# A hybrid decoder layer: bias table as one row a head, the first norm's squares off GpSimd, recurrence constants later

## The chip, the core and the metric

The kernel runs on one core of a Trainium2 chip. Its engines are TensorE (PE, matrix products into PSUM), VectorE (DVE), ScalarE (ACT), GpSimd (POOL) and SyncE (SP, which here only issues transfers); they run in parallel and wait for one another by semaphores. Each takes its own instructions strictly in their order. The metric is the device time of one execution in microseconds. The time before is 2371.75 us, the median of three runs (2360.15 to 2379.61).

## The reference, cut to what matters

```python
def reference(x, ...):
    x = x + 0.5 * swiglu(rms_norm(x, ffn1_norm), w_gate, w_up, w_down)      # FFN 1, D=2048, D_FF=5504
    x = x + hybrid_mixer(rms_norm(x, mix_norm), w_in, ...)                  # RG-LRU beside sparse attention
    x = x + 0.5 * swiglu(rms_norm(x, ffn2_norm), ...)                       # FFN 2
    return rms_norm(x, final_norm)

# in the attention, 16 heads of 128, 256 tokens:
bias = rel_bias[t5_causal_bucket(pos - idx)]     # 32 buckets x 16 heads, by relative position
logits = where(valid, q @ k * scale + bias, lowest)

# in the RG-LRU:
log_a = -8.0 * r * softplus(-lam)                # the constants softplus(-lam) do not depend on x
```

All values are float32; one sequence of 256 tokens.

## The kernel before, in words

Activations lie with the channels on partitions (16 row tiles of 128) and the 256 tokens along the free dimension. For full accuracy each weight and each activation is split into a high part and a low part. A weight tile group is 128 x 1024 (eight row tiles, 512 KB): SP loads it into `raw` (3 buffers, L84), ACT writes the high part `whi` (L68), DVE subtracts and writes the low part `wlo` (L69; 3 buffers of each pair), and for each row tile PE makes one 512-wide matmul with the high part (L111) and one 256-wide one with the low part (L112). These two matmuls are called a pair below. So PE needs a new group every eight pairs, and SP, ACT and DVE work ahead by at most three groups. An SP load waits for its `raw` buffer, and what SP issues later stands behind it.

The layer is FFN 1, the mixer (indexer, keys, values, queries with the attention beside them, RG-LRU, gates, output) and FFN 2. FFN 1 runs over 43 column blocks `j` of 128: a gate product `pg` and an up product `pu`, each 16 pairs long; block 0 mixes them by eight row tiles (gate, up, gate, up), because the input tiles `x1hl` are made on the way. `ready1` (L297) makes input tile c: for three of four tiles ACT multiplies the high part (L71) and DVE the low part (L72), for every fourth tile DVE makes both (L300, L301). The sum of squares of the first norm (`Norm.add`, L160) squares 12 of 16 tiles on GpSimd and 4 on ACT, adds on GpSimd, and `sums` (L172) takes it to PE after block 1's gate product; `rstd` spreads the result, and only then can the waiting blocks be evacuated.

`prepare` (L323) stands after block 4 in the program. Its first part makes the recurrence constants `SP2`, `SN4` and `hb` from `vecs` by some thirty operations on 128 x 16 (tile `st`). Its second part multiplies one-hot buckets by the bias table (L354), which gives for each of 16 heads a row `u` of 384 biases by relative position, and writes it to DRAM (`toep`, L358) as a whole Toeplitz block of 128 x 256 for each head, 2 MB from 16 partitions. The mixer reads it back as `TB` in eight transfers (L413), two heads each, and `logits` adds it to the mask on GpSimd (L493, L494).

Order: a scheduler sets each engine's order from the dependences, so an operation without an early dependence can stand far ahead of its place in the program. `held` (L148) makes a zero that is known only when a product is done, to keep later work back.

Of the kernel before, what the change touches and what calls it, by code (L numbers as in the profile page):

```python
# [18 lines left out]
P = 128  # L19
# [24 lines left out]
def hybrid_layer(ctx: ExitStack, tc: tile.TileContext, a, out):  # L44
# [13 lines left out]
    # ---------------------------------------------------------------- helpers  # L58
# [6 lines left out]
    def split(hi, lo, src, scale=None):  # L65
        """hi + lo == src * scale, each in the tensor engine's one-pass form."""
        if scale is None:
            A.activation(hi, src, AF.Copy)  # L68
            V.tensor_tensor(lo, src, hi.bitcast(F32), op=ALU.subtract)  # L69
        else:  # L70
            A.activation(hi, src, AF.Copy, scale=scale)  # L71
            V.scalar_tensor_tensor(lo, src, scale, hi.bitcast(F32), op0=ALU.mult, op1=ALU.subtract)  # L72

    class Stream:
        """Row tiles of a weight in the order of their use, G to a load, cut in two parts."""
# [29 lines left out]
    def part(ps, w, k0, k1, kts, xs):  # L105
        """Row tiles k0..k1 of kts. xs(kt) -> [P, 2 * S] with the two parts of a row tile side by
        side. Left half: high parts; right half: the mixed terms."""
        for k in range(k0, k1):
            x = xs(k)
            hi, lo = w.pop()  # L110
            T.matmul(ps, hi, x, start=(k == 0), stop=False)  # L111
            T.matmul(ps[:, S:], lo, x[:, :S], start=False, stop=(k == kts - 1))  # L112
# [6 lines left out]
    def product1(w, kts, xs):  # L119
        """All terms in the left half."""  # L120
# [9 lines left out]
    def total(ps, M=P):  # L130
        """The sum of both halves."""
# [16 lines left out]
    def held(ps):  # L148
        """A zero that is known once a product is: it keeps later work off an engine until then."""
# [4 lines left out]
    class Norm:  # L154
        """Sums of squares over the channels, tile by tile, then 1 / rms on every partition."""
# [4 lines left out]
        def add(self, t, pool=False):  # L160
            sq = t1("sq")
            if pool:
                GP.tensor_tensor(sq, t, t, op=ALU.mult)
            else:
                A.activation(sq, t, AF.Square)
# [6 lines left out]
        def sums(self, last=None):  # L172
            """1 / rms with the tokens on partitions; last: squares not yet in the sum."""
# [11 lines left out]
            # One Newton step on the table's root.  # L185
# [5 lines left out]
        def spread(self, after=None):  # L191
            """The same on every partition, in PSUM; not before the product after."""
# [16 lines left out]
    # -------------------------------------------------------------- constants  # L209
# [3 lines left out]
    GP.memset(mean, 1.0 / D)  # L213
    vecs = const.tile([P, 8, KT], F32, name="vecs")
# [3 lines left out]
    # ------------------------------------------------------------------- FFN  # L218
    def ffn(wg, wu, wd, xhl, norm, finish, ready=None, early=None, last=None):
# [14 lines left out]
        for j in range(NF):  # L234
# [16 lines left out]
            if j == 0 and ready is not None:  # L251
                for c in range(KT):
                    norm.add(xr[:, c, :], pool=c < 12)
            if j == 1:
                r = norm.rstd(pg)
            if j == 4 and early is not None:
                early()
# [39 lines left out]
    def ready1(c):  # L297
        if c % 4 == 0:
            hi, lo, g = x1hl[:, c, :S], x1hl[:, c, S:], G1[:, c:c + 1]
            V.tensor_scalar(hi, xr[:, c, :], g, None, op0=ALU.mult)  # L300
            V.scalar_tensor_tensor(lo, xr[:, c, :], g, hi.bitcast(F32), op0=ALU.mult, op1=ALU.subtract)  # L301
        else:
            spread(x1hl, c, xr[:, c, :], G1)
# [17 lines left out]
    toep = dram.tile([HEADS, P, S], F32, name="toep")  # L321

    def prepare():  # L323
        # softplus(-lambda): max(-lam, 0) + log1p(e), e = exp(-|lam|), log1p(e) = 2 artanh(e / (2 + e)).
        st = const.tile([P, 6, KT], F32, name="st")
        neg, e, q_, s_, s2, ac = (st[:, i, :] for i in range(6))
        V.tensor_scalar(neg, LAM, -1.0, None, op0=ALU.mult)
# [13 lines left out]
        for k in range(17, 1, -2):  # L341
# [5 lines left out]
        V.tensor_scalar(hb[:, 0, :], BA, 0.5, None, op0=ALU.mult)  # L347
        V.tensor_scalar(hb[:, 1, :], BX, 0.5, None, op0=ALU.mult)

        # Bias by relative position, as rows of a Toeplitz matrix per head.  # L350
# [6 lines left out]
        uw = u[:HEADS, :]  # L357
        nc.sync.dma_start(toep, bass.AP(tensor=uw.tensor, offset=uw.offset + P - 1,  # L358
                                        ap=[list(uw.ap[0]), [-1, P], [1, S]]))
# [3 lines left out]
    # ----------------------------------------------------------------- mixer  # L363
# [18 lines left out]
    # Indexer.  # L382
# [28 lines left out]
    for i in range(8):  # L411
        normed(first[i] if i < 2 else product(W, KT, xs2), r2, IQ[:, i, :])
        nc.sync.dma_start(TB[:, 2 * i:2 * i + 2, :], toep[2 * i:2 * i + 2].rearrange("h q j -> q h j"))  # L413
# [72 lines left out]

    def logits(h):
# [5 lines left out]
        GP.tensor_tensor(tm[:, :P], TB[:, h, P:], MK[:, :P], op=ALU.add)  # L493
        GP.tensor_tensor(tm[:, P:], TB[:, h, :], MK[:, P:P + S], op=ALU.add)  # L494
# [57 lines left out]
    # RG-LRU. With t = tanh(m / 2), m = -log a: a = 2 y - 1, sqrt(1 - a * a) = 2 sqrt(t) y, y = 1 / (1 + t).  # L552
# [5 lines left out]
    def gates():  # L558
# [12 lines left out]
        # One Newton step on (1 + exp(-m)) / 2; y becomes -1 / (1 + t).  # L571
# [77 lines left out]
    # ------------------------------------------------------- FFN, final norm  # L649
# [27 lines left out]
def _buckets():  # L677
    """One-hot buckets of the relative positions 255 - i, i = 0..383 (negative ones as 0)."""
    n = np.maximum(S - 1 - np.arange(3 * P), 0)
# [7 lines left out]
def _tiles(w):  # L687
    """[K, N] -> [groups of G row tiles, 128 (K inside a tile), G * 128], column tile by column tile."""
# [56 lines left out]
```

## Time and profile before

| | |
|---|---|
| median of three runs | 2371.75 us (2360.15 to 2379.61) |
| span of the profiled execution | 2371.8 us |
| PE busy | 2327.9 us, 98% |
| PE weight loads busy | 2037.1 us, 86% |
| DVE busy | 1514.5 us, 64% |
| ACT busy | 1152.8 us, 49% |
| POOL busy | 120.2 us, 5% |
| moved by DMA | 439.54 MB, 185 GB/s in the mean |

An engine's busy share is a mean over all stages. PE is near its limit almost everywhere, so the places that count are those where it is not; the page cuts the span into 40 slices of 59.3 us, and the chain of work that ended last tells what PE waited for. [...]

### The profile page before, as it was taken

To read this page: it belongs to the slowest core of one execution; us is meant where nothing else is said; L and a number is where in the kernel's file an instruction comes from. 1 tells how busy PE (TensorE), PEld (TensorE's weight loads), DVE (VectorE), ACT (ScalarE), POOL (GpSimd) and SP (SyncE) were. 2 spreads that over 40 slices of the span, in tenths; PEclk is the share of its full clock that TensorE was granted. 3 is DMA by queue.
4 is the path that set the end of the run, shared out by engine and by line. 5 is a ranking of instruction groups with operands and counts; after the bars stand their busy time and mean duration, and the time that the engine had idled before them with its cause. 6 is when DMAs were issued, how large, how long until landed. Compare 5 with 4: busy or idle time off the path is not lost.

```text
span 2371.8 us, 34709 instructions
## 1 busy us (share of the span) xinstructions
PE 2327.9 (98%) x13507; PEld 2037.1 (86%) x13507; DVE 1514.5 (64%) x2236; ACT 1152.8 (49%) x1684; POOL 120.2 (5%) x165
## 2 busy tenths in 40 slices
PE   7799999999999999999999999999999999999998
PEld 6688888888888888899888888888888888888887
DVE  7466666665555687778875566676666666664444
ACT  5344444444444445577654444454544444444442
POOL 4000000000000002100000000021000000000000
PEclk9899999999999999999999999999999999999999
DMA  5755555556655644454565656566666666566564
GB/s 198 169 182 186 186 188 186 186 186 196 196 192 193 220 148 160 147 171 157 181 196 188 191 189 188 196 206 201 187 187 191 190 190 191 189 189 193 188 191 146
DMA packets 130580, 439.54 MB, mean 185 GB/s; under 512 B 14416, under 2 KB 25008, under 8 KB 130416
## 3 DMA queue, kind: packets, MB, share of 16 engines
q1 hardware_dynamic: 129360, 434.94, 57.8%
q8 instruction: 105, 1.72, 0.3%
q0 software_dynamic: 912, 2.33, 0.3%
q14 instruction: 59, 0.48, 0.1%
q10 hardware_dynamic: 144, 0.07, 0.0%
HBM read 430.92 MB, written 6.29 MB: 184 GB/s over the span
## 4 chain that ended last, share of the span: by engine, by line
PE 94%; DVE 2%; DMA 2%; ACT 1%; issue 0%; POOL 0%; SPq 0%; DVEq 0%; ACTq 0%
PE mm L111 58%; PE mm L112 30%; PE mm L126 1%; PE mm L125 1%; PE mm L127 1%; DMA raw<-in_wg 1%; DVE wlo L69 1%; DMA raw<-in_w_rg 1%; ACT whi L68 1%; PE aux L426 0%; DVE x1hl L72 0%; PE aux L561 0%; PE aux L562 0%; DVE hst L608 0%; PE aux L491 0%
## 5 line engine op out<-in xcount | busy, mean ns | idle before, releaser
L69 DVE TENSOR_TENSOR wlo<-raw,whi 128x1024 fp32r<-128x1024 f32 (+2 forms) x807 | 988.0, 1224 | 750.9 <-ACT whi L68 748.5
L68 ACT ACTIVATE whi<-raw 128x1024 fp32r<-128x1024 f32 (+2 forms) x807 | 854.2, 1059 | 1144.0 <-PE mm L111 729.4
L111 PE MATMUL mm<-x1hl,whi 128*128 128x512 f32 x1376 | 494.9, 404 | 22.6 <-ACT whi L68 20.6
L111 PE MATMUL mm<-x3hl,whi 128*128 128x512 f32 x1376 | 477.6, 391 | 0.0
L111 PE MATMUL mm<-h,whi 128*128 128x512 f32 x1333 | 466.8, 395 | 0.0
L111 PE MATMUL mm<-x2hl,whi 128*128 128x512 f32 x1280 | 452.8, 396 | 0.0
L112 PE MATMUL mm<-x1hl,wlo 128*128 128x256 f32 x1376 | 390.7, 284 | 5.4 <-DVE wlo L69 5.2
L112 PE MATMUL mm<-x3hl,wlo 128*128 128x256 f32 x1376 | 385.3, 280 | 0.0
L112 PE MATMUL mm<-h,wlo 128*128 128x256 f32 x1333 | 373.8, 280 | 0.0
L112 PE MATMUL mm<-x2hl,wlo 128*128 128x256 f32 x1280 | 359.2, 281 | 4.0 <-DVE wlo L69 3.9
L111 PEld LDWEIGHTS mm<-x1hl,whi 128*128 128x128 f32 x1376 | 262.8, 191 | 89.8 <-ACT whi L68 20.9
L111 PEld LDWEIGHTS mm<-x3hl,whi 128*128 128x128 f32 x1376 | 257.4, 187 | 56.7
L111 PEld LDWEIGHTS mm<-h,whi 128*128 128x128 f32 x1333 | 249.9, 187 | 58.6
L111 PEld LDWEIGHTS mm<-x2hl,whi 128*128 128x128 f32 x1280 | 239.8, 187 | 54.2 <-issue 0.7
L112 PEld LDWEIGHTS mm<-x1hl,wlo 128*128 128x128 f32 x1376 | 263.9, 192 | 7.2 <-DVE wlo L69 7.2
L112 PEld LDWEIGHTS mm<-x3hl,wlo 128*128 128x128 f32 x1376 | 260.0, 189 | 0.0
L112 PEld LDWEIGHTS mm<-h,wlo 128*128 128x128 f32 x1333 | 251.9, 189 | 0.0
L112 PEld LDWEIGHTS mm<-x2hl,wlo 128*128 128x128 f32 x1280 | 241.8, 189 | 7.2 <-DVE wlo L69 6.3
L135 DVE TENSOR_TENSOR tt<-mm,tb 128x256 f32<-128x256 f32 x285 | 119.0, 418 | 6.0 <-ACT tb L133 6.0
L133 ACT ACTIVATE tb<-mm 128x256 f32<-128x256 f32 x285 | 104.2, 366 | 4.4 <-DVE zero L151 2.2
L142 DVE TENSOR_TENSOR tz<-tt,rstd 128x256 f32<-128x256 f32 x224 | 95.0, 424 | 7.0
L111 PE MATMUL mm<-mg,whi 128*128 128x512 f32 x256 | 90.6, 399 | 0.0
(192 smaller groups left out, 2014.2 us busy)
## 6 DMA issues: line engine op xcount, KB each, us to landing
raw<-in_wu SPq DMA_DIRECT2D x172, 512.0 KB, 4.3
raw<-in_wd SPq DMA_DIRECT2D x172, 512.0 KB, 4.2
raw<-in_wg SPq DMA_DIRECT2D x171, 512.0 KB, 4.3
raw<-in_w_q SPq DMA_DIRECT2D x32, 512.0 KB, 3.5
raw<-in_w_rx SPq DMA_DIRECT2D x32, 512.0 KB, 3.5
raw<-in_w_rg SPq DMA_DIRECT2D x32, 512.0 KB, 3.6
raw<-in_w_ga SPq DMA_DIRECT2D x32, 512.0 KB, 3.6
raw<-in_w_pa SPq DMA_DIRECT2D x32, 512.0 KB, 3.6
```

The lines of the kernel that those rows point to most:

```text
L68: A.activation(hi, src, AF.Copy)
L69: V.tensor_tensor(lo, src, hi.bitcast(F32), op=ALU.subtract)
L111: T.matmul(ps, hi, x, start=(k == 0), stop=False)
L112: T.matmul(ps[:, S:], lo, x[:, :S], start=False, stop=(k == kts - 1))
L125: T.matmul(ps[:, :S], hi, x[:, :S], start=(k == 0), stop=False)
L126: T.matmul(ps[:, :S], hi, x[:, S:], start=False, stop=False)
L127: T.matmul(ps[:, :S], lo, x[:, :S], start=False, stop=(k == kts - 1))
L133: A.activation(b[:M], ps[:M, S:], AF.Copy)
L135: V.tensor_tensor(t[:M], ps[:M, :S], b[:M], op=ALU.add)
L142: V.tensor_tensor(o, t, r, op=ALU.mult)
```

## The change

Five edits, beside removed comments:

- `toep` is kept as 384 values for each head (24 KB, written from ACT's queue); the shift by one position for each query row is made when the rows are read back: partition p reads 256 values from position 1 + p. The bucket table now ascends, so a row lies backwards, and GpSimd reads it with step -1 (`back`).
- The first norm's squares are made by ACT, four row tiles at a time, after block 0's gate product (`add_all` with `held`), and added by DVE in halves; GpSimd has no part in it.
- `ready1` makes all 16 tiles on ACT and DVE together.
- `prepare` gets a `held` zero from block 4's gate product, so that its operations can't stand earlier.
- One small activation (`warm`) brings ACT's first table load forward.


```diff
+        def add_all(self, x, after):
+            sq = hl_tile("sqs", F32, (P, KT, S))
+            z = held(after)
+            for c in range(0, KT, 4):
+                A.activation(sq[:, c:c + 4, :], x[:, c:c + 4, :], AF.Square, bias=z)
+            half = KT
+            while half > 2:
+                half //= 2
+                V.tensor_tensor(sq[:, :half, :], sq[:, :half, :], sq[:, half:2 * half, :], op=ALU.add)
+            self.acc = tmp.tile([P, S], F32, name="sqsum", bufs=1)
+            V.tensor_tensor(self.acc, sq[:, 0, :], sq[:, 1, :], op=ALU.add)
...
+    warm = const.tile([P, 1], F32, name="warm")
+    A.activation(warm, mean, AF.Copy)
...
             if j == 0 and ready is not None:
-                for c in range(KT):
-                    norm.add(xr[:, c, :], pool=c < 12)
+                norm.add_all(xr, pg)
...
             if j == 4 and early is not None:
-                early()
+                early(pg)
...
     def ready1(c):
-        if c % 4 == 0:
-            hi, lo, g = x1hl[:, c, :S], x1hl[:, c, S:], G1[:, c:c + 1]
-            V.tensor_scalar(hi, xr[:, c, :], g, None, op0=ALU.mult)
-            V.scalar_tensor_tensor(lo, xr[:, c, :], g, hi.bitcast(F32), op0=ALU.mult, op1=ALU.subtract)
-        else:
-            spread(x1hl, c, xr[:, c, :], G1)
+        spread(x1hl, c, xr[:, c, :], G1)
...
-    toep = dram.tile([HEADS, P, S], F32, name="toep")
-
-    def prepare():
+    toep = dram.tile([HEADS, 3 * P], F32, name="toep")
+
+    def prepare(after):
+        z = held(after)
...
-        V.tensor_scalar(neg, LAM, -1.0, None, op0=ALU.mult)
+        V.tensor_scalar(neg, LAM, -1.0, z, op0=ALU.mult, op1=ALU.add)
...
-        uw = u[:HEADS, :]
-        nc.sync.dma_start(toep, bass.AP(tensor=uw.tensor, offset=uw.offset + P - 1,
-                                        ap=[list(uw.ap[0]), [-1, P], [1, S]]))
+        nc.scalar.dma_start(toep, u[:HEADS])
...
-        nc.sync.dma_start(TB[:, 2 * i:2 * i + 2, :], toep[2 * i:2 * i + 2].rearrange("h q j -> q h j"))
+        rows = toep[2 * i:2 * i + 2]
+        nc.sync.dma_start(TB[:, 2 * i:2 * i + 2, :],
+                          bass.AP(tensor=rows.tensor, offset=rows.offset + 1,
+                                  ap=[[1, P], list(rows.ap[0]), [1, S]]))
...
+    def back(row):
+        n = row.shape[1]
+        return bass.AP(tensor=row.tensor, offset=row.offset + n - 1, ap=[list(row.ap[0]), [-1, n]])
...
-        GP.tensor_tensor(tm[:, :P], TB[:, h, P:], MK[:, :P], op=ALU.add)
-        GP.tensor_tensor(tm[:, P:], TB[:, h, :], MK[:, P:P + S], op=ALU.add)
+        GP.tensor_tensor(tm[:, :P], back(TB[:, h, :P]), MK[:, :P], op=ALU.add)
+        GP.tensor_tensor(tm[:, P:], back(TB[:, h, :]), MK[:, P:P + S], op=ALU.add)
...
-    n = np.maximum(S - 1 - np.arange(3 * P), 0)
+    n = np.maximum(np.arange(3 * P) - P, 0)
```

How the order on the engines moves (line numbers of the changed kernel are up to 15 higher).

DVE at the start, before: between the low parts of the input tiles (L72, L301) and of the weight groups (`wlo`) stand the operations of `prepare` on `st` and the whole tiles made here (L300).

```order
14 L72 SCALAR_TENSOR_TENSOR x1hl<-xr,vecs,x1hl 128x256 x2
15 L330 TENSOR_SCALAR st<-st 128x16
16 L300 TENSOR_SCALAR x1hl<-xr,vecs 128x256
17 L331 RECIPROCAL st<-st 128x16
18 L69 TENSOR_TENSOR wlo<-raw,whi 128x1024
19 L301 SCALAR_TENSOR_TENSOR x1hl<-xr,vecs,x1hl 128x256
20 L72 SCALAR_TENSOR_TENSOR x1hl<-xr,vecs,x1hl 128x256 x3
21 L300 TENSOR_SCALAR x1hl<-xr,vecs 128x256
22 L72 SCALAR_TENSOR_TENSOR x1hl<-xr,vecs,x1hl 128x256
```

DVE at the start, now, from its first instruction to the end of the squares' additions (`sqs`, `sqsum`); `zero` is the held one.

```order
1 L72 SCALAR_TENSOR_TENSOR x1hl<-xr,vecs,x1hl 128x256 x2
2 L69 TENSOR_TENSOR wlo<-raw,whi 128x512 x2
3 L72 SCALAR_TENSOR_TENSOR x1hl<-xr,vecs,x1hl 128x256 x6
4 L69 TENSOR_TENSOR wlo<-raw,whi 128x1024
5 L72 SCALAR_TENSOR_TENSOR x1hl<-xr,vecs,x1hl 128x256 x8
6 L69 TENSOR_TENSOR wlo<-raw,whi 128x1024 x3
7 L151 TENSOR_SCALAR zero<-mm 128x1
8 L169 TENSOR_TENSOR sqs<-sqs 128x2048
9 L69 TENSOR_TENSOR wlo<-raw,whi 128x1024
10 L169 TENSOR_TENSOR sqs<-sqs 128x1024
11 L69 TENSOR_TENSOR wlo<-raw,whi 128x1024
12 L169 TENSOR_TENSOR sqs<-sqs 128x512
```

The operations on `st` and the whole tiles are gone from here, each weight group's low part stands right behind the tiles it needs, and the sixth weight group's low part (row 9) stands behind an addition of 2048 columns.

ACT in the same place, now: the squares stand behind three weight groups and ahead of five.

```order
6 L71 ACTIVATE x1hl<-xr,vecs 128x256 x6
7 L68 ACTIVATE whi<-raw 128x1024
8 L71 ACTIVATE x1hl<-xr,vecs 128x256 x8
9 L68 ACTIVATE whi<-raw 128x1024 x3
10 L165 ACTIVATE sqs<-xr,zero 128x1024 x4
11 L68 ACTIVATE whi<-raw 128x1024 x5
12 L193 ACT_TABLE_LOAD
```

Before, three single squares of 128 x 256 stood here between the loads' high parts.

SP's queue around the table's write, before: it stands between two weight loads of block 7.

```order
26 L84 DMA raw<-in_wu 128x1024 x2
27 L84 DMA raw<-in_wg 128x1024
28 L358 DMA toep<-u 2048x1x256
29 L84 DMA raw<-in_wg 128x1024
30 L84 DMA raw<-in_wu 128x1024 x2
```

Now the write stands on ACT's queue, between a total (L133) and a weight group's high part, and SP's loads follow each other without it.

```order
46 L68 ACTIVATE whi<-raw 128x1024
47 L133 ACTIVATE tb<-mm 128x256
48 L364 DMA toep<-u 16x384
49 L68 ACTIVATE whi<-raw 128x1024
50 L68 ACTIVATE h<-h 128x256
```

PE's order differs in its first 140 rows only; from there on every engine's order is the old one, apart from operations of `prepare` between blocks 4 and 6.

## Rows read from the trace of the kernel before

**Rows 1.** The page: busy us by engine; PE's busy tenths and granted clock in 40 slices.
```profile
PE 2327.9 (98%) x13507; PEld 2037.1 (86%) x13507; DVE 1514.5 (64%) x2236; ACT 1152.8 (49%) x1684; POOL 120.2 (5%) x165
...
PE   7799999999999999999999999999999999999998
...
PEclk9899999999999999999999999999999999999999
```

**Rows 2.** The page: the chain that ended last, shares by engine and by line.
```profile
PE 94%; DVE 2%; DMA 2%; ACT 1%; issue 0%; POOL 0%; SPq 0%; DVEq 0%; ACTq 0%
PE mm L111 58%; PE mm L112 30%; PE mm L126 1%; PE mm L125 1%; PE mm L127 1%; DMA raw<-in_wg 1%; DVE wlo L69 1%; DMA raw<-in_w_rg 1%; ACT whi L68 1%; PE aux L426 0%; DVE x1hl L72 0%; PE aux L561 0%; PE aux L562 0%; DVE hst L608 0%; PE aux L491 0%
```

**Rows 3.** The chain in order of time: start, duration, what.
```profile
80.96 25.40 DMA raw<-in_wg
```

**Rows 4.** Timeline of SP's queue: start, duration, line, transfer.
```profile
79.83 0.70 SPq L358 DMA_DIRECT2D toep<-u  x1
```

**Rows 5.** DMA issues from 60 to 120 us: size, median us to landing.
```profile
raw<-in_wu SPq DMA_DIRECT2D x8, 512.0 KB, 4.4
...
toep<-u SPq DMA_DIRECT2D x1, 2048.0 KB, 24.5
```

**Rows 6.** Timeline of PE around the stall; idle before and releaser in brackets.
```profile
91.62 0.40 PE L111 MATMUL mm<-x1hl,whi 128*128 128x512 f32 x1
...
93.03 0.40 PE L111 MATMUL mm<-x1hl,whi 128*128 128x512 f32 x1
...
107.55 0.79 PE L111 MATMUL mm<-x1hl,whi 128*128 128x512 f32 x1 [14.01 <-ACT whi L68]
...
114.71 0.39 PE L111 MATMUL mm<-x1hl,whi 128*128 128x512 f32 x1
```

**Rows 7.** Stage: length, busy PE, PEld, DVE, ACT, POOL, granted clock, DMA share, GB/s.
```profile
98.00:100.00 2.00, 0.00 (x0) 0.00 (x0) 0.00 (x0) 0.00 (x0) 0.00 (x0) 0.50 0.83 94
```

**Rows 8.** Timeline of DVE at the start.
```profile
6.36 0.48 DVE L72 SCALAR_TENSOR_TENSOR x1hl<-xr,vecs,x1hl 128x256 fp32r<-128x256 f32 x1
6.76 0.68 DVE L69 TENSOR_TENSOR wlo<-raw,whi 128x512 fp32r<-128x512 f32 x1
...
8.61 1.70 DVE L72 SCALAR_TENSOR_TENSOR x1hl<-xr,vecs,x1hl 128x256 fp32r<-128x256 f32 x2
...
15.57 1.59 DVE L69 TENSOR_TENSOR wlo<-raw,whi 128x1024 fp32r<-128x1024 f32 x1
...
24.80 1.21 DVE L69 TENSOR_TENSOR wlo<-raw,whi 128x1024 fp32r<-128x1024 f32 x1
...
32.20 1.22 DVE L342 SCALAR_TENSOR_TENSOR st<-st 128x16 f32<-128x16 f32 x6
```

**Rows 9.** Timeline of PE at the start.
```profile
26.07 0.58 PE L112 MATMUL mm<-x1hl,wlo 128*128 128x256 f32 x1 [3.52 <-DVE wlo L69]
...
29.01 0.43 PE L111 MATMUL mm<-x1hl,whi 128*128 128x512 f32 x1
...
38.58 0.50 PE L178 MATMUL aux<-mean,sqsum 128*128 128x1 f32 x4
```

**Rows 10.** Timeline of ACT at the start.
```profile
7.96 2.30 ACT L71 ACTIVATE x1hl<-xr,vecs 128x256 fp32r<-128x256 f32 x5
...
10.63 1.06 ACT L68 ACTIVATE whi<-raw 128x1024 fp32r<-128x1024 f32 x1 [0.26 <-DMA raw<-in_wu]
```

**Rows 11.** Reads of the table (line 413): time to landing; ACT's timeline during them.
```profile
DMA to landing us min/median/max: 4.1/5.0/6.0
...
799.86 1.06 ACT L68 ACTIVATE whi<-raw 128x1024 fp32r<-128x1024 f32 x1 [2.21 <-DMA raw<-in_w_iq]
```

**Rows 12.** GpSimd's addition (line 494): duration ns min/median/max, starts; a stretch of attention.
```profile
L494 POOL TENSOR_TENSOR misc<-qT,misc x16: 720/738/1791, 897.0 to 989.7; 128x256 f32<-128x256 f32 x16
...
930.00:950.00 20.00, 20.00 (x121) 17.61 (x120) 14.63 (x36) 11.68 (x25) 3.48 (x6) 1.00 0.47 159
```

**Rows 13.** A steady stretch of FFN 1, columns as in rows 7.
```profile
120.00:180.00 60.00, 60.00 (x342) 52.05 (x341) 38.33 (x54) 28.95 (x43) 0.00 (x0) 1.00 0.56 186
```

More of the change, by code (lines that the diff above doesn't have):

```diff
@@ L158, in __init__, with add @@
             self.name, self.acc = name, None
-        def add(self, t, pool=False):
+        def add_all(self, x, after):
[9 more added lines that the diff above has]
+            V.tensor_tensor(self.acc, sq[:, 0, :], sq[:, 1, :], op=ALU.add)
+        def add(self, t):
             sq = t1("sq")
-            if pool:
-                GP.tensor_tensor(sq, t, t, op=ALU.mult)
-            else:
-                A.activation(sq, t, AF.Square)
+            A.activation(sq, t, AF.Square)
             if self.acc is None:
@@ L297, in ready1 @@
     def ready1(c):
-        if c % 4 == 0:
-            hi, lo, g = x1hl[:, c, :S], x1hl[:, c, S:], G1[:, c:c + 1]
-            V.tensor_scalar(hi, xr[:, c, :], g, None, op0=ALU.mult)
-            V.scalar_tensor_tensor(lo, xr[:, c, :], g, hi.bitcast(F32), op0=ALU.mult, op1=ALU.subtract)
-        else:
-            spread(x1hl, c, xr[:, c, :], G1)
+        spread(x1hl, c, xr[:, c, :], G1)
     n2 = Norm("n2")
@@ L346, in prepare @@
         V.tensor_scalar(SN4, SP2, -2.0, None, op0=ALU.mult)
-        V.tensor_scalar(hb[:, 0, :], BA, 0.5, None, op0=ALU.mult)
-        V.tensor_scalar(hb[:, 1, :], BX, 0.5, None, op0=ALU.mult)
+        V.tensor_scalar(hb[:, 0, :], BA, 0.5, z, op0=ALU.mult, op1=ALU.add)
+        V.tensor_scalar(hb[:, 1, :], BX, 0.5, z, op0=ALU.mult, op1=ALU.add)
         bk = t2("bk", 3 * P)
```

## The prediction

> **What bounds the kernel now.** I read the page first, then the chain in order of time, then engine timelines of the places where the chain leaves TensorE. The page says TensorE (PE) is busy 98% of the span [rows 1], and the chain that ended last is 94% PE, nearly all of it the two matmul lines of `part` [rows 2]. So a change elsewhere is worth something only where PE stands still or runs at its lower clock. The slices show where that is: only the first two of the 40 read a PE share of 7; the granted clock is a digit lower in the second. Two causes lie there.
>
> The first is a stall around 100 us. The Toeplitz write is issued on the SP queue at 79.83 us [rows 4], takes 24.5 us for 2 MB, and every weight load normally lands after 4.4 us [rows 5]. The load issued right behind it lands 25.4 us later and stands on the chain [rows 3]. While it runs, the queue moves 94 GB/s and the clock has fallen to 0.50, the lower of its two levels [rows 7]. PE starves from 93.54 us, 13.7 us after the write was issued, until 107.55 us [rows 6].
>
> The second is the start. VectorE (DVE) is on the chain there: GpSimd squares beside it from 4 us on, and a 1024-wide subtraction takes 1.59 us at 15.57 against 1.21 at 24.80, a 256-wide operation 0.85 us at 8.61 against 0.48 at 6.36 [rows 8]. PE waits 3.52 us for the weight split that ends at 26.0 us, reaches the faster cadence at 29.01 and closes its 48th pair (one 512-wide and one 256-wide matmul) at 38.58 us [rows 9].
>
> **The change part by part.** I count against the span of the profiled execution, 2371.8 us, which is the median of the three runs (2371.75).
>
> *The write of 2 MB goes.* A pair costs (93.03-91.62)/4 = 0.352 us at the higher clock. Between 93.54 and 114.71 us, when the fast cadence is back, PE made 10 pairs [rows 6], worth 3.5 us. The rest, 21.2-3.5 = **17.7 us**, is the stall with its slow matmuls; it goes, because a 24 KB write (16 rows of 1.5 KB) on ACT's queue replaces it and no load stands behind that. What ACT pays is one issue of at most 0.7 us (what the SP issue took [rows 4]) plus a wait for the copy of `u`; ACT is busy 28.95 of 60 us in the steady stage [rows 13], so it is covered. Bounds: 17.7 if all goes, 0 if the load behind still waits.
>
> *The start.* DVE loses GpSimd as a neighbour, four 256-wide multiplications, the small operations of `prepare` up to there; ACT takes the four multiplications. I name the weight groups of eight row tiles g0 (gate), g1 (up), g2, g3 (block 0), g4 to g7 (block 1). The data come as before, so g1 is there at 10.6 us [rows 10]. By ACT at 0.46 us a tile and 1.06 us a group, its order gives g1 split by 11.8, eight tiles by 15.5, g2 by 16.5. DVE follows: low part of g1 till 13.0, eight tiles at 0.45 us till 16.6, low part of g2 at 1.2 till **17.8** us, where it was 26.0. From there 32 pairs at 0.352 us make 11.3 us: 29.1. One new wait comes on top. The squares now wait for the gate product, 24 pairs, closed at T = 20.6 us. ACT needs four squares of 1024 columns, 4 x 1.06, and then DVE the first halving addition of 2048 columns: 512 took 0.68 and 1024 took 1.21 [rows 8], so 2.3 us. Behind it on DVE stands the low part of g5, 1.2 us: ready at T+8.0, while PE, having done g3 and g4, wants it at T+5.6. The stall is 2.4 us and pair 48 ends near 31.5 instead of 38.6. Gain **7.0 us**. Bounds: 5.8 if PE shows again the slow pairs that it had from 26.07 to 29.01 (worth 12.5-11.3 = 1.2 us); 2 if the squares and the additions push a second group late as well. I take 7.0, since PE now has work without a gap from about 13 us on.
>
> *The sum of squares later.* The remaining additions (1024, 512, 256 columns: 1.2, 0.7, 0.4 us) lie between weight splits; the sums move 7 pairs back on PE, the diagonal follows at about T+18, and the block that needs the freed PSUM buffer starts at about T+22. Nothing waits; without the 4 us of cover it would cost what is missing.
>
> *`prepare` after block 4's gate product.* Thirty-three operations of 16 columns at 1.22/6 = 0.20 us [rows 8] and a copy, some 7 us, now stand among three to four weight splits; DVE has 60-38.3 of 60 us free [rows 13], 1.0 us in each group of 2.8 us, that is 3 to 4 us, and two groups lie split ahead of PE. I price it **+0.3 us**, bounds 0 and 3.5 (what does not fit, all shown to PE).
>
> *Reading the rows back shifted.* Eight reads of 256 KB land in 4.1 to 6.0 us, and during them one load came late enough to make ACT wait 2.21 us, which PE did not feel [rows 11]. Below: no change. Above: all 2 MB at the write's 94 GB/s, 22 us. The first five (1.25 MB) would block 13.9 us; the write let PE run dry after 13.7; about 3 us of stall, 4 us more for the three that lie between loads, 2 for the clock: **+9**. I take 0, since the reads are nearest to the old reads: same size, same 128 destination rows, same 1 KB runs; only the start within the row is new.
>
> Why the write was slow decides this. The row shows 2 MB from 16 partitions at 94 GB/s. [...]
>
> *Reading backwards on GpSimd.* The 256-wide addition takes 0.74 us [rows 12] and the 128-wide one less; one head is due each 6.2 us (16 starts from 897.0 to 989.7). Step -1 in place of +1: I take no change; the upper bound is a rival.
>
> *Warm-up activation:* the table load leaves ACT's path (1.3 us), but the second half of g0 lands only at 7.3 us: 0.
>
> Sum: -17.7 - 7.0 + 0.3 = -24.4, so **2347.4 us**, 1.0% less.
>
> **Rivals.** *The reads inherit the stall:* the unaligned, overlapping rows are read at the write's rate. For it: every earlier access with an odd start in this trace is that slow write. Against: its 16 source partitions. 2347.4+9 = 2356. *The start gives little:* the chain of squares holds back g5 and g6, or the clock is still low, and 5 us of the 7 are lost: 2352. For it: DVE and ACT are in order, and the splits stand behind the additions. Against: g6 is only 1.2 us of DVE away. *The stall stays* since the write was slow for its queue, not its bytes: only the start is gained, 2365. Against: 94 GB/s fit 2 MB in 24.5 us. *Slower:* GpSimd's reversed read. It decides where the two additions of a head outlast the head's 6.2 us, against about 1.2 us now; at seven times the price, 8.4 us, PE waits 2.2 us in each of 16 heads, 35 us, which gives 2382. Against: nothing in the trace but the absence of a reversed operand; DVE, at 14.63 of 20 us there [rows 12], would suffer as well.
>
> **How the numbers follow.** Forecast 0.66 (2341 to 2353, from the bounds of the start and `prepare`, and about half a per cent of scatter, as the three runs show); reads slow 0.10; start gives little 0.16; stall stays 0.04; GpSimd 0.04. The range 2336 to 2360 takes in the first three and leaves out the last two and the tails. A measurement tells about 1% from no change; 1% faster is 2348.0, inside the forecast: 0.37 of its 0.66 falls below, and 0.07 of the start's and the reads' cases by scatter. Faster 0.44, within 1% 0.52, slower 0.04 (GpSimd).
>
> **What would show it.** In the profile after: no load above about 8 us near 80 us, PE busy without a gap and clock 1.00 from 60 to 118 us; the second low weight part ending near 18 us; pair 48 near 31.5 us with one wait for a weight split of about 2 us ahead of it; no wait of PE among the small operations near 60 to 75 us; reads of the table landing within 7 us and GpSimd's 256-wide addition at 0.74 us. A PE wait near 800 us, or a GpSimd addition of several us, would make the prediction wrong.

## The result and the profile after

| | before | after |
|---|---|---|
| median of four runs | 2371.1 us (2360.15 to 2379.61) | 2342.93 us (2337.04 to 2343.66) |
| ratio, 95% interval | | 0.9897 (0.9856 to 0.9937) |
| span of the profiled execution | 2371.8 us | 2341.3 us |

The forecast was 2347.4, the range 2336 to 2360: the time fell inside, 28 us (1.2%) less than before where 24.4 were expected. The profiled execution lost 30.5 us of span. The page of after stands against [rows 1]: PE is busy 12 us less with the same 13507 matmuls, the first two slices have risen to 8 and 9, and the granted clock of the second is a 9.

```profile
PE 2316.1 (99%) x13507; PEld 2024.9 (86%) x13507; DVE 1505.7 (64%) x2238; ACT 1156.6 (49%) x1689; POOL 95.0 (4%) x137
...
PE   8999999999999999999999999999999999999998
...
PEclk9999999999999999999999999999999999999999
```

**The stall is gone.** Two stretches of after, in the columns of [rows 7]: the slice that held the stall and the very stretch from 93.54 to 114.71 us of [rows 6]. PE is busy throughout and its clock is 1.00.

```profile
59.30:118.60 59.30, 59.30 (x339) 51.06 (x338) 41.66 (x82) 28.28 (x44) 0.00 (x0) 1.00 0.54 187
93.54:114.71 21.17, 21.17 (x124) 18.53 (x123) 13.38 (x19) 10.79 (x16) 0.00 (x0) 1.00 0.56 191
```

The DMA issues of after from 60 to 120 us answer to [rows 5]: the table's write is 24 KB and lands in 2.0 us, and no load is late.

```profile
raw<-in_wg SPq DMA_DIRECT2D x11, 512.0 KB, 3.4
raw<-in_wu SPq DMA_DIRECT2D x10, 512.0 KB, 3.4
toep<-u ACTq DMA_DIRECT2D x1, 24.0 KB, 2.0
```

**The start is shorter, with a wait and a fall of the clock in it.** DVE's timeline of after answers to [rows 8]: the low part of g2 ends at 16.28 + 1.23 = 17.5 us (it was 26.0). The squares follow at 20.6 on ACT, and the first halving addition takes 2.29 us; the next low weight part stands behind it.

```profile
13.11 3.25 DVE L72 SCALAR_TENSOR_TENSOR x1hl<-xr,vecs,x1hl 128x256 fp32r<-128x256 f32 x8
16.28 1.23 DVE L69 TENSOR_TENSOR wlo<-raw,whi 128x1024 fp32r<-128x1024 f32 x1
...
20.42 0.16 DVE L151 TENSOR_SCALAR zero<-mm 128x1 f32<-128x1 f32 x1
24.92 2.29 DVE L169 TENSOR_TENSOR sqs<-sqs 128x2048 f32<-128x2048 f32 x1 [4.34 <-ACT sqs L165]
27.13 1.22 DVE L69 TENSOR_TENSOR wlo<-raw,whi 128x1024 fp32r<-128x1024 f32 x1
```

PE's timeline of after, the two waits behind the squares and the pairs that follow, answers to [rows 9]:

```profile
26.83 0.50 PE L111 MATMUL mm<-x1hl,whi 128*128 128x512 f32 x1 [0.44 <-ACT whi L68]
...
28.40 0.39 PE L112 MATMUL mm<-x1hl,wlo 128*128 128x256 f32 x1 [1.06 <-DVE wlo L69]
...
30.43 0.63 PE L111 MATMUL mm<-x1hl,whi 128*128 128x512 f32 x1
...
31.07 0.63 PE L111 MATMUL mm<-x1hl,whi 128*128 128x512 f32 x1
...
34.49 0.50 PE L188 MATMUL aux<-mean,sqsum 128*128 128x1 f32 x4
...
73.15 0.81 PE L361 MATMUL aux<-bk,rb 32*16 32x384 f32 x2
```

The last row is the bias matmul, the product of buckets and bias table in `prepare`, recorded as two pieces. It stands behind everything that the change moved at the start, and started at 78.40 before:

```profile
78.40 0.81 PE L354 MATMUL aux<-bk,rb 32*16 32x384 f32 x2
```

About 1 us after the second wait the pairs stretch to 0.64 us. Of the stretches from 28 to 34 us (length, PE busy, granted clock, DMA share, GB/s) the middle one is at 0.50 throughout, its neighbours in part; the traces of before and after grant PE 1.00, full speed, or 0.50 and no third level. The 48th pair is done at 32.1 us (38.6 before, 31.5 predicted).

```profile
28.00:30.00 2.00, 1.60 (x8) 0.88 0.21 66
30.00:32.00 2.00, 2.00 (x7) 0.50 0.68 238
32.00:34.00 2.00, 2.00 (x10) 0.77 0.82 274
```

**The reads and GpSimd, which cost nothing** (against [rows 11, 12]): the eight reads of the table, line 420, land in 4.2 to 7.1 us, and the reversed addition, line 508, has the median of before.

```profile
DMA to landing us min/median/max: 4.2/5.9/7.1
```
```profile
L508 POOL TENSOR_TENSOR misc<-qT,misc x16: 724/735/1779, 861.3 to 954.2; 128x256 f32<-128x256 f32 x16
```

**Something that no step named.** PE is busy without a gap at clock 1.00 in each of these stretches, yet it starts a different number of matmuls. First the kernel before, then after; the columns are length, PE busy with its matmuls, clock, DMA share, GB/s.

```profile
200.00:700.00 500.00, 500.00 (x2832) 1.00 0.58 189
1200.00:1500.00 300.00, 300.00 (x1733) 1.00 0.61 192
1700.00:2200.00 500.00, 500.00 (x2886) 1.00 0.61 190
```
```profile
200.00:700.00 500.00, 500.00 (x2886) 1.00 0.58 194
1200.00:1500.00 300.00, 300.00 (x1699) 1.00 0.60 186
1700.00:2200.00 500.00, 500.00 (x2886) 1.00 0.60 190
```

A pair takes 2 x 500/2886 = 0.3465 us in one case and 2 x 500/2832 = 0.3531 in the other. Measured from first to last start the two cadences are 0.3467 and 0.3533 us, in every trace of this study: each stretch of hundreds of us holds one of the two. I call them quick and slow. The first FFN (200 to 700 us) was slow before and is quick after; the gates (1200 to 1500 us) the other way round.

The matmuls are the same in number and order, so the start of the i-th of them can be compared in the two traces, but for the few that the later sums displace. After minus before, in us:

```
first matmul                  -0.6
bias matmul behind block 4    -5.3   start                     -5.3
matmul 500 (stall past)      -23.6   stall (and 0.5 cadence)  -18.3
matmul 4000 (end of FFN 1)   -35.3   cadence in FFN 1         -11.7
matmul 6250 (attention past) -35.5                             -0.2
matmul 9000 (gates past)     -29.0   cadence in the gates      +6.5
matmul 13500                 -30.3   cadence in w_out          -1.4
```

So some 23 us came by the two steps of the prediction, and 7 net by cadence.

### The profile page after: what moved, and what is told of

The parts are those of the page before. It is cut to its first block, busy times and chain, and to the rows that moved or that the text cites. A ratio compares the mean times of both kernels' runs of the same rounds, so it can differ in the third digit from the quotient of the medians.

```text
span 2341.3 us, 34677 instructions
## 1 busy us (share of the span) xinstructions
PE 2316.1 (99%) x13507; PEld 2024.9 (86%) x13507; DVE 1505.7 (64%) x2238; ACT 1156.6 (49%) x1689; POOL 95.0 (4%) x137
## 4 chain that ended last, share of the span: by engine, by line
PE 94%; DVE 3%; DMA 1%; ACT 1%; issue 1%; SPq 0%; POOL 0%; DVEq 0%; ACTq 0%
PE mm L111 58%; PE mm L112 29%; PE mm L126 2%; PE mm L125 2%; PE mm L127 2%; DVE wlo L69 1%; DMA raw<-in_w_rg 1%; ACT whi L68 0%; DMA raw<-in_wu 0%; PE aux L435 0%; PE aux L575 0%; PE aux L576 0%; DVE hst L622 0%; PE aux L505 0%; DMA raw<-in_wg 0%
## 5 line engine op out<-in xcount | busy, mean ns | idle before, releaser
L111 PE MATMUL mm<-x1hl,whi 128*128 128x512 f32 x1376 | 482.5, 397 | 8.1 <-DVE x1hl L72 7.4
L112 PE MATMUL mm<-x1hl,wlo 128*128 128x256 f32 x1376 | 384.2, 279 | 1.8 <-DVE wlo L69 1.8
L133 ACT ACTIVATE tb<-mm 128x256 f32<-128x256 f32 x285 | 104.2, 366 | 2.0 <-DVE zero L151 2.0
L111 PE MATMUL mm<-yat,whi 128*128 128x512 f32 x256 | 91.2, 399 | 0.0
```

The lines of the kernel that those rows point to most:

```text
L133: A.activation(b[:M], ps[:M, S:], AF.Copy)
```

## The experiments

**The two halves apart.** The table alone, from the kernel before:

```diff
-    toep = dram.tile([HEADS, P, S], F32, name="toep")
+    toep = dram.tile([HEADS, 3 * P], F32, name="toep")
...
-        nc.sync.dma_start(toep, bass.AP(tensor=uw.tensor, offset=uw.offset + P - 1,
-                                        ap=[list(uw.ap[0]), [-1, P], [1, S]]))
+        nc.scalar.dma_start(toep, u[:HEADS])
```
(with the shifted reads and GpSimd's reversed ones of the change), and the rest alone, from the kernel after, with the old write, reads and additions put back.

> The kernel before with the bias table edit alone (24 KB write from ACT's queue, shifted reads, backwards additions); squares, prepare and input tiles as before. Theory (the stall is worth 17.7 us, and the loop of pairs keeps one of two cadences, 0.3466 or 0.3533 us a pair, that each interruption of PE sets anew): no wait near 100 us, pair 48 still closed near 38.6 us, span 2371.8-17.7 = 2354, with up to 13 us either way by the cadence in FFN 1 and the gates. Rival (the table edit itself is worth the 30 us, the start nothing): 2342 with a start as before, in every run. Rival (the whole 12 us of faster cadence in FFN 1 comes from the start's edits): slow cadence throughout FFN 1, 2354 or more.

> The changed kernel with the old bias table (2 MB written from 16 partitions on SP's queue, old reads, forward additions); the edits of the start stay. Theory: start gains 5 us as in the changed kernel, the stall of 17.7 us is back near 95 us, span about 2371.8-5 = 2366, with up to 13 us either way by the cadence. Rival (the stall shrinks because the start left more loads ahead): a wait of PE clearly under 14 us, span under 2360.

The table alone: 2360.81 us median, 0.9975 of before (0.995 to 0.9999). The rest alone: 2364.99, 0.9994 (0.9964 to 1.0024). By medians neither half brings much; by their traces each does what it should. With the table alone no stall is left, and the matmuls behind it start 17.8 us earlier against before, matmul 250 to matmul 500. With the rest alone the bias matmul comes 5.9 us earlier and the stall is back in full. The rows: the table alone in two stretches, then PE of the rest alone.

```profile
86.00:114.00 28.00, 28.00 (x161) 1.00 0.54 187
200.00:700.00 500.00, 500.00 (x2832) 1.00 0.55 189
```
```profile
101.65 0.80 PE L111 MATMUL mm<-x1hl,whi 128*128 128x512 f32 x1 [14.29 <-ACT whi L68]
```

The kernel with the table alone ran its first FFN slow (x2832), the rest alone, in its one trace, quick (x2886 in the same stretch). None of the ten runs of the table alone was below 2353.87; before, of which some runs reached 2355, scatters over 25 us, and the rest alone over 22 (2352.4 to 2374.0). Most of these runs have no trace, so how much of the scatter is cadence is not shown; but a difference of two medians can hold it, and a step has to be read where it happens.

**The changed kernel once more**, unchanged, beside those two:

> The changed kernel, not altered, once more. Theory of the two cadences: places in order of instructions as before, but the stretches with 0.3533 us a pair need not be the same ones; if the gates (about 2050 matmuls) are fast this time the span is 7 us shorter, 2334; if FFN 1 is slow it is 13 us longer, 2354. Rival (the cadence is fixed by the program: addresses, buffers, order): every stretch has the cadence of the first profile, span within 1 us of 2341.

2343.27 us (2340.39 to 2343.94), 0.9893 (0.9846 to 0.9941). Its trace has the first FFN quick again and the gates slow again, but not all of it is the same: w_out, quick in the first trace (232 matmuls from 1570 to 1610 us), is slow in this one (228). So the program alone does not fix the cadence everywhere.

**Why the write was slow.** Two kernels from before, each with an edit to the 2 MB write: its source on 128 partitions instead of 16 (`u2`, a 128 x 256 tile that one DVE operation behind block 4 makes for it), or its 128 copies all from the row's start. Both leave out the right bias values.

```diff
-        nc.sync.dma_start(toep, bass.AP(tensor=uw.tensor, offset=uw.offset + P - 1,
-                                        ap=[list(uw.ap[0]), [-1, P], [1, S]]))
+        nc.sync.dma_start(toep.rearrange("h q j -> q h j"), u2[:, None, :].to_broadcast([P, HEADS, S]))
```
```diff
-        nc.sync.dma_start(toep, bass.AP(tensor=uw.tensor, offset=uw.offset + P - 1,
-                                        ap=[list(uw.ap[0]), [-1, P], [1, S]]))
+        nc.sync.dma_start(toep, bass.AP(tensor=uw.tensor, offset=uw.offset,
+                                        ap=[list(uw.ap[0]), [0, P], [1, S]]))
```

> The kernel before, with one edit: the 2 MB Toeplitz write takes its bytes from a 128x256 tile, repeated for the 16 heads, instead of from the 16 rows of u (so the bias values are left out). Same queue, same place, same 2 MB, same 1 KB runs at the destination. Theory A (the write was slow because its source lies on 16 partitions): it lands in 5 to 8 us instead of 24.5, no weight load near 80 to 110 us takes over 12 us, TensorE has no gap there, and the matmuls behind it start some 17 us earlier. Theory B (2 MB on the weights' queue cost this much from any partitions): landing near 24 us, the gap of 14 us stays.

> The kernel before, with one edit: the 2 MB write still comes from the 16 rows of u, but each of the 128 copies starts at the row's start (offset 0, step 0) instead of one element earlier each time, so that every run of 1 KB begins at the same aligned place (the bias values are wrong by it). Theory A (16 source partitions set the rate): landing stays at 24 to 25 us, 94 GB/s, and TensorE's gap of 14 us stays. Theory B (the odd starts set the rate): landing at 5 to 12 us and no gap.

The write among the DMA issues from 60 to 120 us, and a stretch while it runs (columns as in [rows 7]), first from 128 partitions, then from 16 with aligned starts:

```profile
toep<-u SPq DMA_DIRECT2D x1, 2048.0 KB, 8.3
```
```profile
81.00:88.00 7.00, 7.00 (x42) 6.06 (x41) 4.69 (x8) 2.69 (x4) 0.00 (x0) 1.00 1.00 307
```
```profile
toep<-u SPq DMA_DIRECT2D x1, 2048.0 KB, 24.0
```
```profile
96.00:100.00 4.00, 0.00 (x0) 0.00 (x0) 0.00 (x0) 0.00 (x0) 0.00 (x0) 0.60 0.90 94
```

The same 2 MB on the same queue at the same place land in 8.3 us from 128 partitions, while PE never stops, and the matmuls behind start 17.8 us earlier than before. From 16 partitions they take 24.0 us with aligned starts and 24.5 with odd ones, 94 GB/s in both, and PE waits 13.86 and 14.01 us. So the odd starts were not the cause, the source on 16 partitions was; the source rows are also read 128 times each in the one case and 16 times in the other, which no run separates from the number of partitions. A write from 128 would have removed the stall without the small table, had the values been laid out on them. What holds a source on 16 partitions to 94 GB/s is not shown.

**Do odd starts make the reads slower?** The changed kernel with the reads at each row's start, which leaves out the right bias values:

```diff
-    offset=rows.offset + 1, ap=[[1, P], list(rows.ap[0]), [1, S]]
+    offset=rows.offset, ap=[[0, P], list(rows.ap[0]), [1, S]]
```

> The changed kernel, with each of the 8 reads of the table starting at the row's start for every partition (offset 0, step 0) instead of one element further for each, so that the bias values are wrong by it. Before, these reads (rows already laid out) landed in 4.1 to 6.0 us, median 5.0; in the changed kernel in 4.2 to 7.1, median 5.9. Theory A (the odd starts make the reads slower): median landing back at about 5.0 us. Theory B (not the starts but what else runs at that time): median stays near 5.9. Both: no wait of TensorE there, time within the scatter of the changed kernel, 2337 to 2344 us.

The landing of its eight reads:

```profile
DMA to landing us min/median/max: 4.2/5.5/7.0
```

5.5 with even starts; with odd ones 5.9 in after, and 5.3 to 6.2 over all nine traces that have them. The odd starts cost nothing that can be seen here. The old reads had medians of 4.4 to 5.3 in four traces; why reads of the small table land a little later, with even starts too, stays open. The time, 2333.18, was the lowest single run of the study, and its trace tells why: the first FFN (0.3467 us a pair, in the table below) and the gates (190 GB/s there, where after moves 185 to 188) were both quick.

**What shortened the start.** The changed kernel with the squares as before, twelve of them on GpSimd from the beginning:

```diff
-                norm.add_all(xr, pg)
+                for c in range(KT):
+                    norm.add(xr[:, c, :], pool=c < 12)
```

> The changed kernel, with the squares of the first norm done as before (twelve of the sixteen on GpSimd from the start on, tile by tile, the sums on GpSimd), the rest as changed. Theory A (GpSimd's work beside VectorE was what made the start slow): VectorE's 1024-wide subtractions below 20 us take about 1.6 us again instead of 1.2, the low part of the weight group g2 ends near 24 us instead of 17.5, and the bias matmul behind block 4 starts some 4 to 5 us later, near 78 us. Theory B (the four multiplications taken from VectorE and the later place of the squares made the gain, not GpSimd): g2's low part ends before 20 us and the bias matmul stays near 73 to 74 us.

The timeline of DVE and that of PE in this kernel:

```profile
15.08 6.57 DVE L72 SCALAR_TENSOR_TENSOR x1hl<-xr,vecs,x1hl 128x256 fp32r<-128x256 f32 x8
```
```profile
23.37 0.58 PE L112 MATMUL mm<-x1hl,wlo 128*128 128x256 f32 x1 [5.06 <-DVE wlo L69]
...
76.39 0.81 PE L365 MATMUL aux<-bk,rb 32*16 32x384 f32 x2
```

With GpSimd beside it the same eight DVE operations take 6.57 us instead of 3.25, PE waits 5.06 us for g2, and the bias matmul comes at 76.39, 3.24 later than after's 73.15. So of the start's 5.3 us, 3.2 came by taking the squares from GpSimd, net of what they cost in their new place (the waits and the fall of the clock above, and the slow cadence ahead of the bias matmul), and 2.0 is the rest (four multiplications moved to ACT, `prepare` moved back). How GpSimd's work slows DVE is not shown. The time, 2352.63, is one run: by its trace 3 us of start and 12 of a slow first FFN, less 7 that quick gates gave back.

**The squares in finer pieces.** To take the wait at 26 to 28 us away, the changed kernel with eight squares of 512 columns, each added to a running sum, placed behind block 1's gate product:

```diff
-            for c in range(0, KT, 4):
-                A.activation(sq[:, c:c + 4, :], x[:, c:c + 4, :], AF.Square, bias=z)
+            for c in range(0, KT, 2):
+                A.activation(sq[:, c:c + 2, :], x[:, c:c + 2, :], AF.Square, bias=z)
+                if c:
+                    V.tensor_tensor(sq[:, :2, :], sq[:, :2, :], sq[:, c:c + 2, :], op=ALU.add)
```

> The changed kernel with the squares of the first norm in eight pieces of 512 columns, each added at once to a running sum of 512 columns, and placed behind block 1's gate product in the program, so that the sixth weight group's low part stands ahead of the additions on DVE. Theory: the wait of PE for that low part (2.5 us near 26 to 28 us, then a stretch at the lower clock, about 1.5 us) is gone or under 1 us, the bias matmul of block 4 comes near 70 us instead of 73.2, span 2341.3-3.5 = 2338, apart from the cadence. Rival (the seven additions of 0.6 us hold the next group back as long): a wait of 2 us or more for the seventh group instead, no gain.

Two stretches of it (columns as in the table of 28 to 34 us above):

```profile
28.00:30.00 2.00, 1.78 (x10) 1.00 0.03 6
200.00:700.00 500.00, 500.00 (x2832) 1.00 0.56 189
```

The clock stays at 1.00, the longest wait there is 0.22 us, and the bias matmul comes 3.0 us before after's. The median is 2350.09 all the same (2341.05 to 2353.91): in the trace the first FFN is slow, and the 3.0 us are gone by about matmul 1250 and 9.2 us lost by matmul 4000. The better start stands in a slower kernel.

**What sets the cadence.** By now the traces showed a pattern: in nearly all of them the pairs ran at one cadence ahead of the bias matmul and at the other behind it. Three kernels follow. The first adds six small matmuls of 256 columns to the first FFN of the changed kernel:

```diff
+                    if early is not None and j in (10, 16, 22, 28, 34, 40):
+                        T.matmul(pe[:, :S], ones, hh, start=True, stop=True)
```

> The changed kernel, with one extra matmul of 256 columns (the ones by the block's hidden tile, never read) after the evacuation of blocks 10, 16, 22, 28, 34 and 40 of the first FFN: it does six more interruptions of the loop of pairs, some 0.3 us of work each, 2 us in all. Theory A (each interruption of the loop sets the cadence anew, 0.3466 or 0.3533 us a pair, which is then kept): the first FFN, all at 0.3466 in the changed kernel, changes its cadence at one or more of the six places, and each stretch of 6 blocks (576 pairs) in the slower one costs 3.9 us. Theory B (the cadence is set by something else, such as where the weight loads stand): all seven stretches stay at 0.3466, and the kernel is only 2 us longer.

Two of its stretches, behind the first small matmul and behind the last:

```profile
150.00:200.00 50.00, 50.00 (x290) 1.00 0.53 190
490.00:700.00 210.00, 210.00 (x1213) 1.00 0.57 198
```

2 x 50/290 = 0.345 and 2 x 210/1213 = 0.346: quick in all seven pieces. My theory A falls as written: an interruption as such does not set the cadence. The other two do the 384-column bias matmul itself a second time, behind block 8, in the changed kernel and in the kernel with the table alone (its operand `bk` gets a buffer of its own, so that it is still there):

```diff
+            if j == 8 and turn is not None:
+                T.matmul(pe[:HEADS, :3 * P], rb, bk[:NBUCKET], start=True, stop=True)
```

> The changed kernel, with the 384-column bias matmul done a second time behind block 8 of the first FFN (its result is never read); some 0.7 us of work. In the traces so far the first FFN behind the bias matmul runs at 0.3466 us a pair throughout in every trace of the changed kernel, and in most traces the cadence before the bias matmul and the one behind it differ. Theory A (the bias matmul between two pairs turns the cadence into the other one, and the loop then keeps it): behind block 8 the pairs take 0.3533 us, 0.0067 x about 1760 pairs = 11.8 us more, median near 2354 to 2356. Theory B (each kernel's cadence there is chance, or set by something else in it): the cadence stays 0.3466 behind block 8, as behind the six 256-column matmuls before, and the median is within 2 us of the changed kernel's, 2343 to 2345.

> The kernel with the small table alone (no stall, start as before), with the same second bias matmul behind block 8. That kernel's first FFN ran at 0.3533 us a pair behind the bias matmul and no run of it was below 2353.9 us (median 2360.8). Theory A (the bias matmul turns the cadence into the other one): 0.3466 us behind block 8, 11.8 us less and 0.7 more, median near 2349 to 2350, and no stage besides changes. Theory B (not turned): 0.3533 stays, median near 2361.

The changed kernel with the second matmul, ahead of it and behind it, then the table alone with it:

```profile
80.00:110.00 30.00, 30.00 (x175) 1.00 0.54 193
130.00:160.00 30.00, 30.00 (x172) 1.00 0.54 178
200.00:700.00 500.00, 500.00 (x2833) 1.00 0.55 190
```
```profile
85.00:115.00 30.00, 30.00 (x172) 1.00 0.52 180
130.00:160.00 30.00, 30.00 (x175) 1.00 0.50 178
200.00:700.00 500.00, 500.00 (x2886) 1.00 0.57 193
```

One small matmul turned the quick FFN slow and the slow one quick, and either stays so to the FFN's end. At matmul 4000 the first is 12.1 us behind after, the second 10.5 us ahead of the kernel with the table alone. The medians moved the right way, less than expected in one and more in the other: 2348.23 (2346.36 to 2349.14) where 2354 to 2356 were expected, with gates that in its trace ran quick (x1733 from 1200 to 1500 us) and gave some 7 us back; and 2345.09 (2342.84 to 2349.93) where 2349 to 2350 were expected, with quick gates in its trace too (x1733), though nothing there was edited. The kernel with the table and one idle matmul, with the start as it was, has a ratio of 0.9879 (0.9851 to 0.9907), no worse than the whole change.

All bias matmuls between two runs of pairs, in us a pair ahead of it and behind it, from the starts of the first and the last matmul of each piece (short pieces are off by up to 0.002):

```
                               ahead    behind
before                         0.3473   0.3547
table alone                    0.3473   0.3534
write from 128 partitions      0.3473   0.3534
write aligned                  0.3473   0.3547
GpSimd squares                 0.3473   0.3534
table, second matmul           0.3473   0.3538   second: 0.3538 -> 0.3467
after                          0.3541   0.3467
after once more                0.3540   0.3467
six small matmuls              0.3540   0.3467
reads aligned                  0.3540   0.3467
after, second matmul           0.3540   0.3471   second: 0.3471 -> 0.3534
rest alone                     0.3540   0.3482
second matmul in the gates     0.3540   0.3467   second: 0.3533 -> 0.3536
finer squares                  0.3533   0.3534
```

15 of 17 turn the cadence: quick became slow seven times of seven, slow became quick eight times of ten, and two left it slow. With the squares of before the piece ahead is quick, with those of the change slow: that is how, in these traces, the change made the first FFN quick. Not every interruption turns it, though: ahead of the second FFN's norm ten of the 14 traces are slow and four quick (w_out's last 200 matmuls), and behind that norm's small matmuls, of 1 and of 128 columns, all 14 are quick, 0.3467, to the end of that FFN.

**A version that uses it.** The gates were slow in the profiles of the changed kernel. The changed kernel with the second bias matmul behind the first tile of the gates:

```diff
         t = total(product(W2, KT, whole(yat)))
+        if n == 0:
+            again()
```

> The changed kernel, with the bias matmul done a second time, now behind the first tile of the gates (w_ga and w_pa) instead of inside the first FFN; the result is never read and the output is unchanged. In the three profiles of the changed kernel and of the one with six small matmuls the gates ran at 0.3533 us a pair from there. Theory A (such a matmul between pairs turns the cadence into the other one there too): the gates run at 0.3466 us from the second tile on, some 1000 pairs x 0.0067 = 6.6 us less and 0.7 more, median near 2336 to 2338 against 2343 of the changed kernel. Theory B (the cadence of the gates is set by something else or by chance from run to run): the median stays at 2342 to 2345, or the runs spread over 7 us as without it.

2338.03 us median (2334.94 to 2343.76), 0.9862 (0.983 to 0.9893). This is the fastest median of several runs in the study, but it does not show its reason. The profiled run was the slowest of the six, and in it the matmul turned nothing:

```profile
1200.00:1500.00 300.00, 300.00 (x1700) 1.00 0.60 187
```

The other runs, 2334.9 to 2342.6, have no trace. Theory B, chance from run to run, is not excluded for the gates (w_out above did differ between two traces of one kernel), and 2338 against 2343 comes from few runs, on another chip than the second measurement of the changed kernel.

## Why the prediction was right, and where it was not

- **The bound** was read rightly: everything gained lies where PE stood still, ran at its lower clock, or (not foreseen) ran its pairs at the slower cadence.
- **The stall, 17.7 us:** 17.8 in the kernel with the table alone. The source on 16 partitions, which the prediction held against the rival of slow reads, was the author's estimate: no row of before shows it as the cause. The two writes bore it out (24.0 us from 16 partitions with aligned starts, 8.3 from 128).
- **The start, 7.0 us:** 6.4 at the 48th pair, where the prediction counted it, and 5.3 at the bias matmul. Up to the wait, step by step it went as worked out: the low part of g2 ends at 17.5 us (17.8 predicted), the gate product closes at 20.4 (20.6), the halving addition takes 2.29 us (2.3), the low part of g5 is ready at 28.4 (28.6). PE's wait there was 0.44 + 1.06 us, less than the 2.4 predicted: it came for g5 at 26.4 us (26.2 predicted) and made one 512-wide matmul between the two waits. The mis-sized term is what came behind the wait. "PE now has work without a gap from about 13 us on" left out the clock: it fell to the lower level, 0.50 in the row of 30 to 32 us, 0.5 to 1.1 us after this wait in after and in three more kernels with this start, while in three others with the same waits it stayed at 1.00. These three finish pair 48 at 30.6 to 31.0 us instead of 32.1 to 32.8, but then PE waits 0.76 to 0.95 us for the norm's diagonal at 38.6 to 38.9, which the four with the fall do not; the bias matmul comes at 72.2 to 72.5 us instead of 73.1 to 73.4. So the fall is worth some 0.9 us at the bias matmul, and does not always come; and "Nothing waits", said of the later sums, holds in after but not in those three. Finer squares, without the wait and without the fall, got 3.0 us back. The slow cadence ahead of the bias matmul, 93 pairs, took another 0.6.
- **`prepare`, +0.3:** no wait of PE among its small operations from 68 to 78 us; it is covered, as said, and bounds up to 3.5 were not needed.
- **Reads, GpSimd's reversed addition, warm-up, all 0:** right for the first two. The reads landed 0.9 us later in the median and PE did not feel it; 735 ns against 738 for the addition. The warm-up can't be told from scatter: the first matmul starts at 6.0 us in after, 6.7 in after once more and 6.6 before.
- **The rivals:** reads that inherit the stall, and a stall that stays, fell with the landing times (4.2 to 7.1 us for the reads, 2.0 for the write); the reversed read fell with the 735 ns. "The start gives little" came a third of the way.
- **The sum, -24.4:** right in its terms, which measured -23.1 (17.8 and 5.3). The profiled 30.5 us are more because some 7 us of cadence, which no term held, came on top; without them the time would have been near 2350, in the range as well. How near it came to the forecast is luck: the first FFN's turn gave 11.7 us and the gates' took 6.5, and neither was foreseen. The step that failed is the price of a pair: 0.352 us was taken from [rows 6] as the price of any pair at the higher clock. It was that of one cadence; the trace of before itself has x2886 in 500 us elsewhere. 1.9% over the first FFN alone, 1904 pairs, is 12.7 us, half the sum. Read ahead of the prediction, it would not have told the sign, but it would have told that the same work at the same clock can differ by half of what was forecast.

## What to carry to other kernels

A transfer whose SBUF side lies on few partitions can be slow, as the 2 MB from 16 were here (94 GB/s and 24.0 us, against 8.3 us from 128): look at its GB/s before you shrink it, since spreading its source may do as much. Read a step's gain where it happens, by the start of the same matmul in both traces: by the traces up to 12 us of a whole run here came by cadence and by no term of the change, enough to set an improvement of 3 us at the start beside a median 7 us longer. Count matmuls in long stretches in which PE is fully busy at full clock; if the counts differ, so does the cadence, and the work that interrupts the loop is a place to look.

## What the hardware showed unexpectedly

- **Two steady cadences at full clock.** A loop of weight loads with a 512- and a 256-column matmul in turn ran at 0.3467 or 0.3533 us a pair, at clock 1.00, PE busy 100%, for up to some 680 us without a change. A 384-column matmul with 16-column weights in between turned one into the other 15 times of 17; a 256-column matmul with 128-column weights left it alone, quick, six times of six, and behind the second FFN's norm it was quick 14 times of 14. What in PE holds the cadence, why two did not turn and why the gates and w_out change between kernels that do the same there, stays open: no row shows weight loads or queues in enough detail, and no other size was tried.
- **DVE beside GpSimd:** 0.82 us for a 256-column multiplication with GpSimd's squares running beside it, 0.41 without them, over eight in a row (6.57 and 3.25 us).
- **The clock's fall is not certain.** The same two waits (0.44 to 0.45 and 1.06 to 1.07 us) were followed by clock 0.50 in four traces and by 1.00 in three. What decides it is not shown.
